# Sums of the out projection's weight blocks: made in SBUF beside the product, or all in DRAM during attention

## The chip, the cores and the metric

The kernel runs on one core of a Trainium2 chip. The metric is the device time of one execution in microseconds (us). PE is the matrix engine, DVE the vector engine, ACT the scalar engine, POOL the GpSimd engine, SP the engine that issues most DMAs; DMA stands for the 16 DMA engines that serve the core.

## The reference, cut to what matters

One layer with sliding-window attention, then a gated embedding and a norm; everything is float32, with 512 tokens and a model width of 2048:

```python
hn = rmsnorm(x, norm_g)
q, k, v, gate = jnp.split(hn @ swa_w_in, ...)
out = attention(q, k, v, window=128, relative bias, sinks)
x = x + (out * jax.nn.silu(gate)) @ swa_w_out        # the out projection
emb = p @ ple_proj
g = jax.nn.sigmoid(rmsnorm(x, ple_norm) @ ple_gate)
x = x + emb * g
return rmsnorm(x, final_g)
```

## The kernel before

**Products.** Each float32 operand is split into a high part (rounded to the type that PE multiplies) and a low part (the rest), and a product is three matmuls: high by high, high by low, low by high. The high part of a weight piece is a cast on ACT (line 668, tile bhi), the low part a subtraction on DVE (line 669, tile blo). A piece is 128 x 1024 floats, 512 KB. The activations' parts are called fho and flo in the out projection (forms, lines 919 and 920).

**Fewer products by sums.** The out projection and the gate product of the embedding (PLE) are made by Strassen's scheme in Winograd's form: seven products of half-sized matrices in place of eight. Weight quarters are written (row, column): product 1 takes quarter (1,1), 2 takes (2,1), 3 takes (2,2), product 7 takes (1,2) + (2,2), 6 takes sum 7 + (1,1), 5 takes (1,1) + (1,2), 4 takes sum 6 + (2,1). The forms of the activations are differences to match. In the out projection the scheme is applied once more inside product 2 and inside product 4: their smaller products are the steps "m" (product 2) and "n" (product 4), seven products of two pieces each.

**Stages.** Until about 60 us the keys, values and first queries are made. From there to about 450 us the query and gate projections run on PE, and from about 100 us the attention of 64 blocks runs between their matmuls. The weight pieces of these projections (tile wraw, 60 of them, three places) are loaded by SP (line 101), cast on ACT (whi, line 107) and subtracted on DVE (wlo, line 113). From 452 to about 617 us stands the out projection, then PLE to the end.

**Sums in DRAM.** While attention runs, `sum_weights(n)` is called, 102 calls spread evenly over the 64 blocks. Even calls issue a copy of a 512 KB piece from DRAM to DRAM on SP (line 627), odd calls a DMA on POOL that adds another piece to that copy (line 629), three pairs later. So are made the sums 7, 5 and 6 of the out projection, sums 7 and 5 of PLE, and the small sums that the steps "m" need: 48 copies and 48 adds.

**Sums in SBUF.** The rest is made during the out projection. Sum 6 is loaded into eight tiles (grown, kind "seed"); four steps after a tile's use a DMA on POOL adds quarter (2,1) to it (`Inside.grow`, line 740), which makes sum 4. Ten more DMAs on POOL (lines 750 and 760) then make the sums for the steps "n" from these tiles, so that those pieces (kind "part") need no load.

**The order.** The list OUT holds the 68 pieces of the out projection in order: large products (tuples) take 12 matmuls a piece, "m" and "n" six. `Pieces.get(i)` returns the split piece i, and through `ahead(i)` issues loads up to a few pieces ahead and splits up to two or three pieces ahead. Raw pieces of kind "one" lie in the three places of wraw (tile braw), those of kind "small" in two tiles beside them, "seed" in grown. Split pieces have three places (bhi, blo); from piece 14 on every fourth piece uses one more, `spare`. On PE and SP the order is that of the program. On DVE, ACT and POOL it is that of the program until the eighth piece (`order.close()`), then a scheduler's.

Of the kernel before, what the change touches and what calls it, by code (L numbers as in the profile page):

```python
# [20 lines left out]
P = 128  # L21
# [34 lines left out]
def trunk_kernel(ctx: ExitStack, tc: tile.TileContext, a: dict):  # L56
# [546 lines left out]
    def small_sum(q, first, more):  # L603
        for i in range(2):
            t = small[q, i] = tc.dram_tile([P, WE], F32, name=f"small_{q}_{i}")
            copies.append((t, first(i)))
            adds.append((t, more(i)))

    small_sum(7, lambda i: small_piece(0, 1, i), lambda i: small_piece(1, 1, i))
    small_sum(5, lambda i: small_piece(0, 0, i), lambda i: small_piece(0, 1, i))  # L610
    for nm, p in SUMS:
        if (nm, p) == ("w_out", 5):
            small_sum(6, lambda i: small[7, i], lambda i: small_piece(0, 0, i))
        if (nm, p) == ("w_out", 6):
            small_sum(4, lambda i: small[6, i], lambda i: small_piece(1, 0, i))
        for jj in range(2):
            for m in range(4):
                t = summed[nm, p, jj, m] = tc.dram_tile([P, WE], F32, name=f"{nm}_{p}_{jj}_{m}")
                first = {7: (1, 2), 5: (1, 1)}.get(p)
                copies.append((t, block(nm, *first, jj, m) if first else summed[nm, 7, jj, m]))  # L620
                adds.append((t, block(nm, *{7: (2, 2), 5: (1, 2), 6: (1, 1)}[p], jj, m)))
    SUM_STEPS = 2 * len(copies) + 6

    def sum_weights(i):

        if i % 2 == 0 and i // 2 < len(copies):
            nc.sync.dma_start(*copies[i // 2])
        elif i % 2 == 1 and 0 <= i // 2 - 3 < len(adds):
            nc.gpsimd.dma_start(*adds[i // 2 - 3], accum_op=ALU.add, max_dma_last_dim=8192)

    class Pieces:
# [3 lines left out]
        def __init__(self):  # L635
            self.specs, self.base, self.made, self.grown, self.due = [], {}, {}, {}, []
            self.aside, self.first4, self.last4 = [], 0, 0
# [4 lines left out]
        def _prepare(self, i):  # L642
            kind, src, key = self.specs[i]
            if kind == "grow":
                t = self.grown[key]
                nc.gpsimd.dma_start(t, src, accum_op=ALU.add)
            else:
                if kind == "seed":
                    t = self.grown[key] = rooms[0].tile([P, WE], F32, tag="grown", name=f"grown{i}", bufs=8)
                elif kind == "small":  # L650
                    n = small_place(key)
                    if key in (0, 2):
                        self.aside.append(rooms[0].tile([P, 2, WE], F32, tag="partial", name=f"small{key}", bufs=2))
                    t = self.aside[n // 2][:, n % 2]
                else:
                    t = wpool.tile([P, WE], F32, tag="wraw", name=f"braw{i}")
                nc.sync.dma_start(t.rearrange("p (k c) -> p k c", k=2) if kind == "proj" else t, src)
            self.base[i] = t

        def _split(self, i):  # L660
            kind, whose, key = self.specs[i]
            raw = whose.raw(*key) if kind == "part" else self.base.pop(i)
# [5 lines left out]
            nc.scalar.copy(hi, raw)  # L668
            nc.vector.tensor_sub(lo, raw, hi.bitcast(F32))  # L669
            self.made[i] = tuple([t[:, :512], t[:, 512:]] for t in (hi, lo))  # L670
            if kind == "part":
                whose.split(*key)
# [11 lines left out]
        def ahead(self, i):  # L684

            last = len(self.specs) - 9
            for n in range(max(i, 0), min(i + 6, last) + 1):
                kind = self.specs[n][0]
                if n in self.base or n < self.done or kind in ("grow", "part"):
# [5 lines left out]
                if kind == "small":  # L695
                    sooner = all(self.specs[v][0] != kind or small_place(self.specs[v][2]) != small_place(self.specs[n][2]) for v in self.base)
                    if not sooner:
                        continue
                if sooner or n <= i + (4 if self.first4 <= i < self.last4 - 2 else 3):
                    self._prepare(n)  # L700
            while self.done <= min(i + (3 if self.first4 <= i < self.last4 - 2 else 2), last):
                self._split(self.done)
                self.done += 1

        def get(self, i):
# [3 lines left out]
            if kind in ("seed", "grow"):  # L709
                n = next((n for n in range(i + 1, len(self.specs)) if self.specs[n][2] == key), None)  # L710
                if n is not None:
                    self.due.append((i + 6, partial_of(self._prepare, n)))
                elif key[0] == inside.nm:
                    self.due.append((i + GROW, partial_of(inside.grow, key)))
# [5 lines left out]
    GROW = 4  # L720
    FIRST_SMALL, LAST_SMALL = 14, 46

    def small_place(key):
        return key % 4 if key < 10 else 2 + key % 2

    FOURTH = 14, 68
# [4 lines left out]
    class Inside:  # L731
# [10 lines left out]
        def begin(self):  # L742

            s7 = rooms[0].tile([P, 2, 2, 512], F32, tag="partial", name="sum7", bufs=2)
            self.s7 = s7.rearrange("p i k c -> p i (k c)")
            self.t = {(kh, jj, i): B.grown[self.nm, jj, 2 * kh + i] for kh in range(2) for jj in range(2) for i in range(2)}

        def sums(self):
            for i in range(2):
                nc.gpsimd.dma_start(self.s7[:, i], self.t[1, 1, i])  # L750
                yield
            for i in range(2):
                self.grow_by(self.s7[:, i], self.t[0, 1, i])
                yield
            for i in range(2):
                self.grow_by(self.t[0, 1, i], self.t[0, 0, i])
                yield

        def grow_by(self, out, more):
            nc.gpsimd.dma_start(out, more, accum_op=ALU.add)  # L760

        def raw(self, q, i):
            if q == 7:
                return self.s7[:, i]
            return self.t[{1: (0, 0), 6: (0, 0), 5: (0, 1), 2: (1, 0), 4: (1, 0), 3: (1, 1)}[q] + (i,)]

        def split(self, q, i):
            if q == 1:
                self.grow_by(self.t[0, 0, i], self.s7[:, i])
            elif q == 2:  # L770
                self.grow_by(self.t[1, 0, i], self.t[0, 0, i])
# [62 lines left out]
    def add_stage(nm, order):  # L834
        at = {}
        if nm == inside.nm:
            parts = [(q, i) for q in ORDER_IN for i in range(2)]
            smalls = [(q, i) for q in ORDER_IN for i in range(2)]
            for step in OUT:
                if step == "m":  # L840
                    q, i = smalls.pop(0)
                    raw = {1: (0, 0), 2: (1, 0), 3: (1, 1)}.get(q)
                    B.add("small", small_piece(*raw, i) if raw else small[q, i], 2 * ORDER_IN.index(q) + i)
                    continue
                if step == "n":
                    B.add("part", inside, parts.pop(0))
                    continue
# [5 lines left out]
                B.add("seed" if p == 6 else "one", src, (nm, jj, m) if p == 6 else None)  # L853
# [113 lines left out]
    for _ in range(2 * 2):  # L967
        while splits(2):
            W.split()
        ksteps(8)  # L970
    for e in range(2):
# [10 lines left out]
    for i in range(blocks + 3):  # L982
# [221 lines left out]
    def turns_of(*v):  # L1204
# [7 lines left out]
    seeds = [n for n, spec in enumerate(B.specs) if spec[0] == "seed" and spec[2][0] == inside.nm]  # L1212
    sooner = {v: n for n, v in enumerate(((1,0,1),(1,0,3)))}
    held, coming = {}, []
    inner_sums, inner_forms = inside.sums(), inside.forms()
    extra = {
        (5, 1, 0): [inside.begin, inner_sums, inner_sums], (5, 1, 1): [inner_forms, inner_sums, inner_sums],
        (5, 1, 2): [inner_forms, inner_sums, inner_sums], (5, 1, 3): [inner_forms], (3, 0, 0): [inner_forms],
# [21 lines left out]
    for at, step in enumerate(OUT):  # L1240
        if at == 8:
# [23 lines left out]
        if step in sooner:  # L1265
            B._prepare(seeds[sooner[step]])
# [305 lines left out]
```

## Time and profile before

| | us |
|---|---|
| runs without a profile | 804.85, 805.84, 804.90 |
| their median | 804.9 |
| the profiled execution | 806.73 |
| its span, from the first to the last instruction | 805.0 |
| PE busy in it | 785.0 |
| DVE, ACT, POOL busy | 612.4, 499.6, 169.8 |

The profile is one execution. PE is busy for 98% of the span, and its matmuls are pipelined, so that time is lost where it sits idle, or where its clock was granted at half. "PE o <- ACT bhi" in the waits means that a matmul which writes o waited for the cast that made bhi. DMA share is the mean busy share of the 16 DMA engines; packets of two queues can overlap, so that it goes a little over 1.

### The profile page before, as it was taken

To read this page: it belongs to the slowest core of one execution; us is meant where nothing else is said; L and a number is where in the kernel's file an instruction comes from. 1 tells how busy PE (TensorE), PEld (TensorE's weight loads), DVE (VectorE), ACT (ScalarE), POOL (GpSimd) and SP (SyncE) were. 2 spreads that over 40 slices of the span, in tenths; PEclk is the share of its full clock that TensorE was granted. 3 is DMA by queue.
4 is the path that set the end of the run, shared out by engine and by line. 5 is a ranking of instruction groups with operands and counts; after the bars stand their busy time and mean duration, and the time that the engine had idled before them with its cause. 6 is when DMAs were issued, how large, how long until landed. Compare 5 with 4: busy or idle time off the path is not lost.

```text
span 805.0 us, 11199 instructions
## 1 busy us (share of the span) xinstructions
PE 785.0 (98%) x3738; PEld 653.1 (81%) x3738; DVE 612.4 (76%) x1043; ACT 499.6 (62%) x1016; POOL 169.8 (21%) x384
## 2 busy tenths in 40 slices
PE   9999999999999999999999999959999999999995
PEld 7888888888888888888888888847788888888885
DVE  4445478888868787687876999848798666899885
ACT  5641367677656666566666658526789755667755
POOL 0003014443243414441234103201100020210000
PEclk9999999999999999999999999989999999999998
DMA  8770598999888978898787479999873996885533
GB/s 332 277 214 6 186 250 226 246 254 244 242 258 218 222 230 216 247 247 243 208 230 171 158 278 332 288 266 351 249 214 101 367 220 218 171 222 189 178 105 105
DMA packets 47338, 180.77 MB, mean 225 GB/s; under 512 B 6880, under 2 KB 7520, under 8 KB 42800
## 3 DMA queue, kind: packets, MB, share of 16 engines
q1 hardware_dynamic: 36992, 134.26, 48.0%
q0 software_dynamic: 10000, 45.41, 29.5%
q8 instruction: 29, 0.48, 0.2%
q10 hardware_dynamic: 288, 0.39, 0.2%
q14 instruction: 29, 0.24, 0.1%
HBM read 168.97 MB, written 54.58 MB: 278 GB/s over the span
## 4 chain that ended last, share of the span: by engine, by line
PE 85%; DMA 7%; DVE 4%; issue 1%; ACT 1%; SPq 0%; DVEq 0%; ACTq 0%
PE qps L124 7%; PE qps L126 7%; PE qps L125 7%; PE gps L124 7%; PE gps L125 7%; PE gps L126 7%; PE g L126 5%; PE g L125 5%; PE g L124 5%; DMA small<-small 4%; PE o L125 3%; DMA grown<-w_out 3%; PE o L126 3%; PE o L124 3%; PE s L401 2%; PE o L523 2%
## 5 line engine op out<-in xcount | busy, mean ns | idle before, releaser
L669 DVE TENSOR_TENSOR blo<-braw,bhi 128x1024 fp32r<-128x1024 f32 x68 | 83.3, 1225 | 32.9 <-ACT bhi L668 32.5
L668 ACT CAST bhi<-braw 128x1024 fp32r<-128x1024 f32 x68 | 71.5, 1053 | 58.9 <-DMA braw<-w_out 16.7
L124 PE MATMUL gps<-xh,whi 128*128 128x512 f32 x256 | 100.5, 393 | 0.0
L125 PE MATMUL gps<-xl,whi 128*128 128x512 f32 x256 | 100.0, 391 | 0.0
L126 PE MATMUL gps<-xh,wlo 128*128 128x512 f32 x256 | 99.9, 390 | 0.0
L503 POOL TENSOR_SCALAR_AFFINE_SELECT own<-r 64x256 fp32r<-64x256 f32 x96 | 60.7, 632 | 184.8 <-ACT r L484 102.5
L113 DVE TENSOR_TENSOR wlo<-wraw,whi 128x1024 fp32r<-128x1024 f32 x60 | 73.5, 1226 | 25.0 <-ACT whi L107 23.6
L124 PE MATMUL qps<-xh,whi 128*128 128x512 f32 x224 | 87.7, 392 | 0.0
L125 PE MATMUL qps<-xl,whi 128*128 128x512 f32 x224 | 87.4, 390 | 0.0
L126 PE MATMUL qps<-xh,wlo 128*128 128x512 f32 x224 | 87.4, 390 | 0.0
L461 ACT ACTIVATE t<-t,sm 128x129 f32<-128x129 f32 x128 | 50.6, 397 | 49.2 <-DVE sm L452 46.4
L124 PE MATMUL g<-bhi,fhg 128*128 128x512 f32 x192 | 75.2, 392 | 0.0
L126 PE MATMUL g<-bhi,flg 128*128 128x512 f32 x192 | 74.8, 390 | 0.0
L125 PE MATMUL g<-blo,fhg 128*128 128x512 f32 x192 | 74.7, 389 | 0.0
L107 ACT CAST whi<-wraw 128x1024 fp32r<-128x1024 f32 x60 | 62.1, 1037 | 15.4 <-DMA wraw<-in_w_q 15.4
L124 PE MATMUL o<-bhi,fho 128*128 128x512 f32 x132 | 52.4, 397 | 7.2 <-ACT bhi L668 7.2
L484 ACT CAST r<-pt 128x256 fp32r<-128x256 f32 x64 | 23.8, 372 | 55.7 <-PE pt L479 55.3
L126 PEld LDWEIGHTS gps<-xh,wlo 128*128 128x128 f32 x256 | 48.1, 188 | 10.6
L124 PEld LDWEIGHTS gps<-xh,whi 128*128 128x128 f32 x256 | 48.1, 188 | 9.0
L125 PEld LDWEIGHTS gps<-xl,whi 128*128 128x128 f32 x256 | 48.1, 188 | 8.7
L125 PE MATMUL o<-blo,fho 128*128 128x512 f32 x132 | 52.7, 400 | 1.6 <-DVE blo L669 1.6
L126 PE MATMUL o<-bhi,flo 128*128 128x512 f32 x132 | 52.0, 394 | 0.0
(276 smaller groups left out, 1893.3 us busy)
## 6 DMA issues: line engine op xcount, KB each, us to landing
wraw<-in_w_gate_in SPq DMA_DIRECT2D x32, 512.0 KB, 5.9
wraw<-in_w_q SPq DMA_DIRECT2D x28, 512.0 KB, 6.1
w_out<-in_w_out POOLq DMA_DIRECT2D x24, 512.0 KB, 7.8
braw<-in_ple_gate SPq DMA_DIRECT2D x24, 512.0 KB, 4.2
w_out<-in_w_out SPq DMA_DIRECT2D x16, 512.0 KB, 8.2
ple_gate<-in_ple_gate SPq DMA_DIRECT2D x16, 512.0 KB, 7.0
ple_gate<-in_ple_gate POOLq DMA_DIRECT2D x16, 512.0 KB, 7.2
braw<-in_w_out SPq DMA_DIRECT2D x16, 512.0 KB, 4.1
```

What stands on the lines that cost most here:

```text
L107: nc.scalar.copy(hi, self.raw[i])
L113: nc.vector.tensor_sub(lo, raw, hi.bitcast(F32))
L124: nc.tensor.matmul(ps, sh, mh, start=first, stop=False, skip_group_check=more)
L125: nc.tensor.matmul(ps, sh, ml, start=False, stop=False, skip_group_check=more)
L126: nc.tensor.matmul(ps, sl, mh, start=False, stop=last, skip_group_check=more)
L401: nc.tensor.matmul(s_ps[:, u, : 2 * n], st, key[:, :, first : first + n], start=True, stop=True)
L461: nc.scalar.activation(su, su, AF.Exp, bias=sm[:, u : u + 1], accum_out=sm[:, 2 + u : 3 + u])
L484: nc.scalar.copy(r[:, 0], PT[i])
L503: nc.gpsimd.affine_select(out=cols(own[places[g % 2 ^ low]]), in_=cols(r[here, low].bitcast(F32)), pattern=[[sign * QB, 2], [0, GROUP], [s ...
L523: nc.tensor.matmul(out, first, r[:, low], start=low == 0, stop=own is None and low == 1)
L668: nc.scalar.copy(hi, raw)
L669: nc.vector.tensor_sub(lo, raw, hi.bitcast(F32))
```

## The change

All sums of the out projection are made in DRAM during attention, those of sum 4 and of the steps "n" too: 62 copies and 64 adds (two of the sums are added in place, into a piece of sum 4 that nothing reads any more). Of the now 134 calls of `sum_weights` eight stand ahead of the attention, and 126 are spread over its 64 blocks. The pieces 4 to 67 are plain loads into a ring of eight places (tile ring, in the space of the grown tiles), up to nine pieces ahead, as places come free. `Inside` keeps only the forms. The extra place `spare` serves from piece 6 on, and the program's order holds on DVE, ACT and POOL to the twentieth piece.

```diff
-    def small_sum(q, first, more):
+    def sum_of(first, more, nm):
+        t = tc.dram_tile([P, WE], F32, name=nm)
+        copies.append((t, first))
+        adds.append((t, more))
+        return t
+    def small_sum(of, q, first, more):
         for i in range(2):
+            small[of, q, i] = sum_of(first(i), more(i), f"small_{of}_{q}_{i}")
+    def large_sum(nm, p, only=range(2)):
+        for jj in only:
             for m in range(4):
+                summed[nm, p, jj, m] = sum_of(
+                    block(nm, *first, jj, m) if first else summed[nm, 7 if p == 6 else 6, jj, m],
+                    block(nm, *{7: (2, 2), 5: (1, 2), 6: (1, 1), 4: (2, 1)}[p], jj, m),
...
+    large_sum("w_out", 5)
+    large_sum("w_out", 4)
+    large_sum("ple_gate", 7, (0,))
+    small_sum(4, 7, lambda i: large_piece(1, 1, i), lambda i: large_piece(0, 1, i))
+    for i in range(2):
+        small[4, 5, i] = large_piece(0, 1, i)
+        copies.append(None)
+        adds.append((small[4, 5, i], large_piece(0, 0, i)))
...
-    SUM_STEPS = 2 * len(copies) + 6
+    SUM_START = 8
+    SUM_REST = 2 * len(copies) + 6 - SUM_START
...
+                elif FIRST_RING <= i < LAST_RING:
+                    t = rooms[0].tile([P, WE], F32, tag="grown", name=f"ring{i}", bufs=8)
...
-            for n in range(max(i, 0), min(i + 6, last) + 1):
+            for n in range(max(i, 0), min(i + REACH, last) + 1):
...
-                if kind == "one" and FIRST_SMALL <= n < LAST_SMALL:
-                    sooner = sum(self.specs[v][0] == "one" for v in self.base) < 3
+                if FIRST_RING <= n < LAST_RING:
+                    sooner = len(rooms) > 0
...
-    FOURTH = 14, 68
+    FIRST_RING, LAST_RING, REACH = 4, 68, 9
+    FOURTH = 6, 68
...
-        def grow(self, key):
-            nm, jj, m = key
-            nc.gpsimd.dma_start(B.grown[key], block(nm, 2, 1, jj, m), accum_op=ALU.add)
...
-        def sums(self):
-            for i in range(2):
-                nc.gpsimd.dma_start(self.s7[:, i], self.t[1, 1, i])
...
-                B.add("seed" if p == 6 else "one", src, (nm, jj, m) if p == 6 else None)
+                B.add("one", src)
...
-            for n in range(i * SUM_STEPS // blocks, (i + 1) * SUM_STEPS // blocks):
-                sum_weights(n)
+            for n in range(i * SUM_REST // blocks, (i + 1) * SUM_REST // blocks):
+                sum_weights(SUM_START + n)
...
-        if at == 8:
+        if at == 20:
             order.close()
```

**SP during attention, around the load of the last block of biases.** A row is a DMA, out<-in, with the program's tile numbers; `w_out_4_1_2` is a piece of sum 4, `small_4_7_0` a small sum for the steps "n". Before:

```order
L101 DMA wraw41_3407<-in_w_gate_in 128x1024
L627 DMA ple_gate_7_0_0_778<-in_ple_gate 16x8192
L101 DMA wraw42_3471<-in_w_gate_in 128x1024
L101 DMA wraw43_3533<-in_w_gate_in 128x1024
L627 DMA ple_gate_7_0_1_779<-in_ple_gate 16x8192
L627 DMA ple_gate_7_0_2_780<-in_ple_gate 16x8192
L101 DMA wraw44_3655<-in_w_gate_in 128x1024
```

and now:

```order
L101 DMA wraw41_3444<-in_w_gate_in 128x1024
L652 DMA ple_gate_7_0_3_789<-in_ple_gate 16x8192
L101 DMA wraw42_3508<-in_w_gate_in 128x1024
L652 DMA small_4_7_0_790<-w_out_4_1_2_784 16x8192
L101 DMA wraw43_3571<-in_w_gate_in 128x1024
L652 DMA small_4_7_1_791<-w_out_4_1_3_785 16x8192
L101 DMA wraw44_3692<-in_w_gate_in 128x1024
```

The copies stand denser between the loads of wraw, and two of those shown here read a sum that POOL's adds finished shortly before.

On POOL the eighteen DMAs of lines 740, 750 and 760 are gone from the out projection; only the four that add the input stay there, ahead of PLE's.

**DVE, at the fourth to seventh piece of the out projection.** `gate` and `fg` are subtractions that make forms, `flo` and `pTl` low parts of forms. Before:

```order
L669 TENSOR_TENSOR blo4_5045<-braw4_5018,bhi4_5044 128x1024
L920 TENSOR_TENSOR flo7_01_5061<-gate0_1697,fho7_01_5060 128x512
L812 SCALAR_TENSOR_TENSOR pTl_4992<-gate2_3998,pTh_4991 128x512
L907 TENSOR_TENSOR gate0_1697<-gate2_3998,gate0_1697 128x4x256
L669 TENSOR_TENSOR blo5_5067<-braw5_5042,bhi5_5066 128x1024
L907 TENSOR_TENSOR gate1_2862<-gate1_2862 128x4x256
L669 TENSOR_TENSOR blo6_5090<-braw6_5064,bhi6_5089 128x1024
```

and now:

```order
L781 TENSOR_TENSOR fg_5034<-gate2_4036,gate3_4629 128x512
L690 TENSOR_TENSOR blo4_5099<-ring4_5045,bhi4_5098 128x1024
L895 TENSOR_TENSOR flo7_01_5115<-gate0_1723,fho7_01_5114 128x512
L690 TENSOR_TENSOR blo5_5121<-ring5_5047,bhi5_5120 128x1024
L882 TENSOR_TENSOR gate1_2896<-gate1_2896 128x4x256
L690 TENSOR_TENSOR blo6_5142<-ring6_5049,bhi6_5141 128x1024
```

One small subtraction moved ahead of piece 4, and two form instructions moved from before piece 5 to later places.

More of the change, by code (lines that the diff above doesn't have):

```diff
@@ L601, in small_piece, with large_piece @@
         return block("w_out", 2, 1, jj, 2 * kh + i)
-    def small_sum(q, first, more):
-        for i in range(2):
[L605 to L616, printed above, removed]
+    def large_piece(kh, jj, i):
+        return summed["w_out", 4, jj, 2 * kh + i]
@@ L619, in trunk_kernel @@
                 first = {7: (1, 2), 5: (1, 1)}.get(p)
-                copies.append((t, block(nm, *first, jj, m) if first else summed[nm, 7, jj, m]))
-                adds.append((t, block(nm, *{7: (2, 2), 5: (1, 2), 6: (1, 1)}[p], jj, m)))
-    SUM_STEPS = 2 * len(copies) + 6
+                summed[nm, p, jj, m] = sum_of(
+                    block(nm, *first, jj, m) if first else summed[nm, 7 if p == 6 else 6, jj, m],
+                    block(nm, *{7: (2, 2), 5: (1, 2), 6: (1, 1), 4: (2, 1)}[p], jj, m),
+                    f"{nm}_{p}_{jj}_{m}",
+                )
@@ new lines, in trunk_kernel @@
+    small_sum(2, 7, lambda i: small_piece(0, 1, i), lambda i: small_piece(1, 1, i))
+    small_sum(2, 5, lambda i: small_piece(0, 0, i), lambda i: small_piece(0, 1, i))
+    large_sum("w_out", 7)
+    small_sum(2, 6, lambda i: small[2, 7, i], lambda i: small_piece(0, 0, i))
+    large_sum("w_out", 6)
+    small_sum(2, 4, lambda i: small[2, 6, i], lambda i: small_piece(1, 0, i))
+    large_sum("w_out", 5)
+    large_sum("w_out", 4)
+    large_sum("ple_gate", 7, (0,))
+    small_sum(4, 7, lambda i: large_piece(1, 1, i), lambda i: large_piece(0, 1, i))
@@ L624, in sum_weights @@
+    for i in range(2):
+        small[4, 5, i] = large_piece(0, 1, i)
+        copies.append(None)
+        adds.append((small[4, 5, i], large_piece(0, 0, i)))
+    large_sum("ple_gate", 7, (1,))
+    small_sum(4, 6, lambda i: small[4, 7, i], lambda i: large_piece(0, 0, i))
+    large_sum("ple_gate", 5, (0,))
+    small_sum(4, 4, lambda i: small[4, 6, i], lambda i: large_piece(1, 0, i))
+    large_sum("ple_gate", 5, (1,))
+    SUM_START = 8
+    SUM_REST = 2 * len(copies) + 6 - SUM_START
     def sum_weights(i):
@@ L626, in sum_weights @@
         if i % 2 == 0 and i // 2 < len(copies):
-            nc.sync.dma_start(*copies[i // 2])
+            if copies[i // 2]:
+                nc.sync.dma_start(*copies[i // 2])
         elif i % 2 == 1 and 0 <= i // 2 - 3 < len(adds):
@@ L636, in __init__ @@
             self.specs, self.base, self.made, self.grown, self.due = [], {}, {}, {}, []
-            self.aside, self.first4, self.last4 = [], 0, 0
+            self.first4, self.last4 = 0, 0
         def add(self, kind, srcs, key=None):
@@ L660, in _split @@
         def _split(self, i):
-            kind, whose, key = self.specs[i]
-            raw = whose.raw(*key) if kind == "part" else self.base.pop(i)
+            raw = self.base.pop(i)
             if self.first4 <= i < self.last4 and i % 4 == 3:
@@ L670, in _split @@
             self.made[i] = tuple([t[:, :512], t[:, 512:]] for t in (hi, lo))
-            if kind == "part":
-                whose.split(*key)
         def split_last(self, k, hi, lo):
@@ L686, in ahead @@
             last = len(self.specs) - 9
-            for n in range(max(i, 0), min(i + 6, last) + 1):
+            for n in range(max(i, 0), min(i + REACH, last) + 1):
                 kind = self.specs[n][0]
-                if n in self.base or n < self.done or kind in ("grow", "part"):
+                if n in self.base or n < self.done or kind == "grow":
                     continue
-                if kind == "one" and FIRST_SMALL <= n < LAST_SMALL:
-                    sooner = sum(self.specs[v][0] == "one" for v in self.base) < 3
+                if FIRST_RING <= n < LAST_RING:
+                    sooner = len(rooms) > 0
                 else:
                     sooner = kind == "seed" and n <= i + 6
[L695 to L699, printed above, removed]
+                if sooner or n <= i + 3:
                     self._prepare(n)
@@ L719, in trunk_kernel @@
     B = Pieces()
[L720 to L724, printed above, removed]
-    FOURTH = 14, 68
+    FIRST_RING, LAST_RING, REACH = 4, 68, 9
+    FOURTH = 6, 68
     FINAL_G = 6
@@ L736, in __init__ @@
             self.nm, self.made = nm, {}
-        def grow(self, key):
-            nm, jj, m = key
-            nc.gpsimd.dma_start(B.grown[key], block(nm, 2, 1, jj, m), accum_op=ALU.add)
[L742 to L746, printed above, removed]
-        def sums(self):
-            for i in range(2):
-                nc.gpsimd.dma_start(self.s7[:, i], self.t[1, 1, i])
[L751 to L771, printed above, removed]
         def forms(self):
@@ L842, in add_stage @@
                     raw = {1: (0, 0), 2: (1, 0), 3: (1, 1)}.get(q)
-                    B.add("small", small_piece(*raw, i) if raw else small[q, i], 2 * ORDER_IN.index(q) + i)
+                    B.add("one", small_piece(*raw, i) if raw else small[2, q, i])
                     continue
                 if step == "n":
-                    B.add("part", inside, parts.pop(0))
+                    q, i = parts.pop(0)
+                    raw = {1: (0, 0), 2: (1, 0), 3: (1, 1)}.get(q)
+                    B.add("one", large_piece(*raw, i) if raw else small[4, q, i])
                     continue
@@ L965, in splits @@
         return len(W.made) <= min(at // 8 + ahead, len(W.srcs) - 1)
-    for _ in range(2 * 2):
+    for n in range(2 * 2):
         while splits(2):
@@ L970, in trunk_kernel @@
         ksteps(8)
+        for v in range(SUM_START // 4):
+            sum_weights(n * (SUM_START // 4) + v)
     for e in range(2):
@@ L1211, in trunk_kernel @@
     smalls = small_forms(small_made)
-    seeds = [n for n, spec in enumerate(B.specs) if spec[0] == "seed" and spec[2][0] == inside.nm]
-    sooner = {v: n for n, v in enumerate(((1,0,1),(1,0,3)))}
     held, coming = {}, []
-    inner_sums, inner_forms = inside.sums(), inside.forms()
+    inner_forms = inside.forms()
     extra = {
-        (5, 1, 0): [inside.begin, inner_sums, inner_sums], (5, 1, 1): [inner_forms, inner_sums, inner_sums],
-        (5, 1, 2): [inner_forms, inner_sums, inner_sums], (5, 1, 3): [inner_forms], (3, 0, 0): [inner_forms],
+        (5, 1, 1): [inner_forms], (5, 1, 2): [inner_forms], (5, 1, 3): [inner_forms], (3, 0, 0): [inner_forms],
         (3, 0, 1): [partial_of(turn, 0, 0, "o")],
@@ L1264, in trunk_kernel @@
             load_x(x_at[step])
-        if step in sooner:
-            B._prepare(seeds[sooner[step]])
         if p in ahead and (p != 5 or seen2 >= 10):
```

8 lines of the change are left out of this document (removed).

## The prediction

> **What bounds the kernel now.** I read the page's first part, then PE by stage, then what PE waited for, and from there backwards.
>
> ```profile
> span 805.0 us, 11199 instructions
> PE 785.0 (98%) x3738; PEld 653.1 (81%) x3738; DVE 612.4 (76%) x1043; ACT 499.6 (62%) x1016; POOL 169.8 (21%) x384
> ```
>
> PE is the bound: whatever is gained must come out of the 20 us in which it is idle, or out of matmuls at a low clock. Busy time by stage (engine us and count, then the granted clock, DMA share and GB/s moved) shows where those are:
>
> ```profile
> core 0: us, PE busy (x) PEld busy (x) DVE busy (x) ACT busy (x) POOL busy (x), PEclk, DMA share, GB/s
> 0.00:60.00 60.00, 58.70 (x295) 49.55 (x296) 27.29 (x41) 33.57 (x44) 3.15 (x10) 1.00 0.82 276
> 60.00:100.00 40.00, 40.00 (x184) 33.28 (x183) 20.25 (x36) 10.93 (x15) 8.52 (x30) 1.00 0.31 97
> 100.00:450.00 350.00, 350.00 (x1737) 293.63 (x1737) 277.81 (x607) 227.78 (x625) 123.60 (x305) 1.00 0.85 231
> 450.00:500.00 50.00, 50.00 (x223) 41.33 (x223) 47.49 (x58) 31.59 (x43) 4.55 (x5) 1.00 0.77 264
> 500.00:530.00 30.00, 30.00 (x134) 24.65 (x133) 24.02 (x28) 16.19 (x20) 8.23 (x9) 1.00 1.07 282
> 530.00:550.00 20.00, 11.15 (x38) 7.72 (x37) 9.21 (x10) 7.59 (x10) 1.10 (x2) 0.74 1.04 319
> 550.00:580.00 30.00, 29.32 (x128) 23.16 (x127) 23.49 (x29) 19.10 (x31) 4.30 (x5) 1.00 0.97 287
> ...
> 620.00:790.00 170.00, 170.00 (x766) 140.99 (x765) 139.02 (x177) 113.17 (x162) 13.79 (x16) 1.00 0.70 202
> 790.00:805.00 15.00, 5.82 (x49) 5.62 (x47) 7.79 (x24) 5.33 (x11) 0.00 (x0) 0.79 0.43 140
> ```
>
> Attention and PLE have no idle PE at all. The start loses 1.3 us and the tail 9.2, which the change leaves alone. Between 530 and 580 us, in the middle of the out projection, PE loses 8.85 + 0.68 = 9.5 us, and its clock drops. What it waited for, of the whole stretch from 100 to 790 us:
>
> ```profile
> PE o L124 <- ACT bhi L668: 7.2, 1, 7.2
> PE o L125 <- DVE blo L669: 2.3, 4, 0.7
> ```
>
> One wait of 7.2 us for a cast, and small ones for the subtraction behind it. In the timeline of PE the matmuls after it start 0.43 us apart:
>
> ```profile
> 541.51 0.80 PE L124 MATMUL o<-bhi,fho 128*128 128x512 f32 x1 [7.21 <-ACT bhi L668]
> ...
> 544.22 0.63 PE L125 MATMUL o<-blo,fho 128*128 128x512 f32 x1
> 544.64 0.63 PE L126 MATMUL o<-bhi,flo 128*128 128x512 f32 x1
> ```
>
> and the clock in two cuts of 5 us there is at half:
>
> ```profile
> 536.00:541.00 5.00, 0.00 (x0) 0.00 (x0) 0.00 (x0) 0.58 (x1) 0.00 (x0) 0.50 1.05 275
> 541.00:546.00 5.00, 4.02 (x9) 2.84 (x10) 2.79 (x3) 2.79 (x4) 0.00 (x0) 0.50 1.03 344
> ```
>
> The cast came late because its raw piece did. ACT in the same stretch sits idle before one cast after the other, each time for a load:
>
> ```profile
> 522.90 1.05 ACT L668 CAST spare<-small 128x1024 fp32r<-128x1024 f32 x1 [1.29 <-DMA small<-in_w_out]
> 526.75 1.05 ACT L668 CAST bhi<-braw 128x1024 fp32r<-128x1024 f32 x1 [2.26 <-DMA braw<-w_out]
> 530.51 1.05 ACT L668 CAST bhi<-small 128x1024 fp32r<-128x1024 f32 x1 [2.71 <-DMA small<-small]
> 540.41 1.04 ACT L668 CAST bhi<-braw 128x1024 fp32r<-128x1024 f32 x1 [8.85 <-DMA braw<-w_out]
> ```
>
> And the loads are late because the DMA engines are full, with POOL's adds into SBUF in the first place. The DMAs issued between 500 and 540 us, by queue (packets, MB, share of the 16 engines) and by issue (median us to landing):
>
> ```profile
> q0 software_dynamic: 1771, 5.17, 66.2%
> q1 hardware_dynamic: 1769, 5.96, 40.2%
> grown<-in_w_out POOLq DMA_DIRECT2D x7, 512.0 KB, 22.2
> braw<-w_out SPq DMA_DIRECT2D x4, 512.0 KB, 24.5
> ```
>
> q0 carries POOL's DMAs, q1 the loads. The two move the same number of packets, but q0's take 66% of the engines. The loads get 5.96 MB in 40 us, 149 GB/s. There the pieces alternate between twelve matmuls and six; 18 matmuls at 134 in 30 us are 4.03 us, and two pieces of 0.524 MB in that time are 260 GB/s. So a load takes 24.5 us, and PE runs out of pieces.
>
> **The change, part by part.** *The stall.* The eight adds into grown and the ten DMAs for the steps "n" leave this stage. By queue, from 450 to 600 us, with one issue:
>
> ```profile
> q1 hardware_dynamic: 8576, 29.89, 53.7%
> q0 software_dynamic: 3503, 10.94, 36.2%
> braw<-in_w_out SPq DMA_DIRECT2D x12, 512.0 KB, 3.9
> ```
>
> A POOL DMA of 0.524 MB costs 150 x 0.362 / 10.94 x 0.524 = 2.6 us of all engines, a load 150 x 0.537 / 29.89 x 0.524 = 1.4. Eighteen of the first go (47 us) and about fourteen loads more come (20 us): 135 us of busy time become 108, in a stage that is then 137 us long, a share of 0.79 where now 1.07 stands for 30 us and more. With eight places each load also has seven pieces' time, 9 to 19 us, to land; the twelve plain loads from in_w_out in these 150 us landed in 3.9. (How many come into the stage more is an estimate from the order of SP.) So I let the stall go whole. In matmuls: at 4.47 per us, 20 us should hold 89.3 and hold 38, and 30 us should hold 134 and hold 128. That is 57.3 matmuls, **12.8 us**; 9.5 of it is idle time, the other 3.3 the half clock. What is late next is DVE.
>
> *DVE's order.* From 450 to 500 us DVE is busy 47.49 of 50 us. The change adds nothing to its work. One subtraction comes ahead of piece 4, form work moves away from piece 5, and the extra place from piece 6 lets splits run further ahead. The nearest rows:
>
> ```profile
> 463.18 0.68 DVE L812 SCALAR_TENSOR_TENSOR pTl<-gate,pTh 128x512 fp32r<-128x512 f32 x1
> 463.78 1.22 DVE L907 TENSOR_TENSOR gate<-gate,gate 128x1024 f32<-128x1024 f32 x1
> ```
>
> One instruction of 0.68 us comes sooner, 1.9 us move back. Bounds: a further gain of 0.5 us (what small waits my count may miss), or a loss if DVE, in written order, waits where the scheduler filled in: four instructions like the second, 4.9 us. I take a loss of 0.4, since both moves are small beside the 2.7 us that PE spends on a piece, and since before piece 20 there was no wait to lose.
>
> *The sums in attention.* This is the price. 14 more copies on SP, 16 more adds on POOL; of these 11 and 15 fall into the 350 us of attention, the rest ahead of it, where the DMA share is 0.31. The queues from 100 to 450 us:
>
> ```profile
> q1 hardware_dynamic: 11152, 55.35, 46.4%
> q0 software_dynamic: 3840, 25.17, 38.3%
> ```
>
> the 50 us of it with the highest share:
>
> ```profile
> 150.00:200.00 50.00, 50.00 (x253) 42.02 (x252) 40.91 (x90) 35.16 (x98) 21.56 (x54) 1.00 0.94 247
> ```
>
> and the loads of wraw, with what they waited for and how long they took:
>
> ```profile
> L107 ACT CAST whi<-wraw x53: 1029/1034/1051, 105.2 to 439.7; 128x1024 fp32r<-128x1024 f32 x53
>   ACT whi L107: 9.9, 15
> DMA to landing us min/median/max: 3.4/6.0/11.6
> ```
>
> An add costs 350 x 0.383 / 48 = 2.8 us of all engines, a copy 350 x 0.464 / 55.35 x 0.524 = 1.54. So 15 x 2.8 + 11 x 1.54 = 59 us are added, and the share goes from 0.85 to 1.02; 1.07 was held in the out projection. In bytes, 231 GB/s become 231 + 26 x 0.524 / 350 = 270, and the row at 1.07 moved 282. It is full, but it fits. What would feel it first are the loads of wraw. A cast comes every 334.5 / 52 = 6.4 us; a load goes out when the piece three before it is split, so 3 x 6.4 less some 2.3 us for cast and subtraction, 17 us, ahead of its use. It lands in 6.0, at worst 11.6: a margin of 11 and 5.4 us. No cast waited for a load (the only wait in the wraw rows is DVE's for ACT). I put this at **nothing**, with the margin as the cover; if that is used up, every further us of lateness is a us of PE, which is the second rival. Below nothing it cannot go, since PE has no idle time there.
>
> SP is in order, so that copies which wait for a sum hold the wraw loads queued behind them. The closest pair is `small_4_7_0`, 5 calls or 2.5 blocks behind its add: 2.5 x 5.5 (350 us for 64 blocks) = 13.7 us against the landing of an add:
>
> ```profile
> ple_gate<-in_ple_gate POOLq DMA_DIRECT2D x16, 512.0 KB, 7.2
> w_out<-in_w_out POOLq DMA_DIRECT2D x24, 512.0 KB, 7.8
> ```
>
> About 6 us to spare there, and a wait would take from a margin of 5 to 11. POOL's own adds stand 3.5 blocks behind their copies instead of 4.4, 19 us against a landing of about 8: behind a waiting add stand the selects of the next block, which PE needs, but there is room.
>
> **Sum.** The profiled execution took 806.7 us: 806.7 - 12.8 + 0.4 = 794.3. It lies 1.8 over the median of the runs, 804.9, so the forecast for the median is 792.5.
>
> **The rivals.** *DVE takes over* (partly faster). For it: 47.49 of 50 us busy at the stage's start. Against it: no PE wait there. Price: four instructions of 1.22 us, 4.9 us at most: 797.
>
> *Attention's transfers do not fit* (slower). Mechanism: adds and copies queue up faster than the 16 engines take them, wraw lands ever later, and PE waits for each piece. For it: the stage's share comes to 1.02, and 0.94 is the most that 50 us of it show, at 247 GB/s. If that is its limit, 270 / 247 x 350 = 383 us of transfers, 33 late, less the median margin of 11: 22 us of PE waits, 792.5 + 22 = 814. Against it: 1.07 in the out projection. It makes the kernel slower from a lateness of 12.4 + 11 = 23 us on, a limit of 270 x 350 / 373 = 253 GB/s.
>
> *The memory, not the engines, is the limit* (slower). Copies and adds touch DRAM at least twice per byte: now 80.5 MB + 25.17 + 47 x 0.524 = 130 MB in 350 us, 372 GB/s, then 27 MB more. If 372 were all, 157 MB would take 422 us, 72 late, less 11: 854. Against it: nothing says that 372 is a ceiling; at 150 to 200 us the engines moved more than the mean, and PE did not wait. The Trainium skill, "DMA: Bandwidth & Descriptors", section Specifications, gives about 358 GB/s of HBM for one core. By that rule the stage would take 157 / 0.358 = 439 us. The trace does not agree: it has carried 372 for 350 us with PE busy throughout.
>
> *It does not do what it says* (no change): the loads are late for another reason, say SP's order, and the stall comes again: 804.9. Against it: equal packets in both queues while q0 holds 66% of the engines.
>
> **How the numbers follow.** Stall gone and all else hidden: 0.64, at 791 to 794.5. DVE takes over, or attention leaks a few us of waits: 0.12, at 795 to 803. No change: 0.04. Transfers do not fit: 0.17, since no stretch of the attention shows a share of 1.02. Memory: 0.03. The time is that of the first. The range must hold 8 in 10: the first two hold 0.76, no change the rest, so 791 to 805.5. About 0.2%, 1.6 us, is what a measurement of this kernel tells from no change. Faster 0.76, same 0.04, slower 0.20.
>
> **What would show it.** Right: no PE wait between 450 and 600 us; q0 almost empty there, loads landing in 4 to 8 us; a DMA share near 1 from 100 to 450 us with PE still busy 350 of 350; wraw landing in 7 to 11 us, no cast waiting for it. Wrong: waits "whi <- DMA wraw" that grow through the attention, followed by PE waits and a clock below 1.00 before 450 us; waits of PE for blo from 455 to 500 us with DVE busy throughout, for the first rival; SP waiting long before `small_4_7_0`, POOL before an add.

## The result and the profile after

The changed kernel takes 792.1 us (median of 6 runs, 791.8 to 792.53), the kernel before 804.96: a ratio of 0.983, 95% interval 0.982 to 0.985. The forecast was 792.5. The first lines of the page of the changed kernel:

```profile
span 790.2 us, 11240 instructions
PE 780.0 (99%) x3738; PEld 652.3 (83%) x3738; DVE 612.9 (78%) x1043; ACT 499.6 (63%) x1016; POOL 175.8 (22%) x382
```

The span is 14.8 us shorter, and PE is idle for 10.2 us in all, at the start and in the tail. The same cuts as before show what happened in between (engine us and count, granted clock, DMA share, GB/s):

```profile
0.00:60.00 60.00, 58.78 (x299) 49.65 (x299) 28.42 (x42) 34.65 (x46) 5.70 (x13) 1.00 0.84 276
60.00:100.00 40.00, 40.00 (x184) 33.32 (x183) 19.60 (x35) 10.66 (x18) 14.01 (x32) 1.00 0.61 185
100.00:450.00 350.00, 350.00 (x1738) 293.81 (x1737) 277.85 (x608) 226.94 (x621) 137.31 (x318) 1.00 0.96 266
...
150.00:200.00 50.00, 50.00 (x254) 42.05 (x253) 40.26 (x90) 34.73 (x97) 22.91 (x52) 1.00 1.02 284
...
450.00:500.00 50.00, 50.00 (x224) 41.36 (x223) 45.11 (x52) 29.77 (x39) 1.48 (x2) 1.00 0.80 270
500.00:530.00 30.00, 30.00 (x134) 24.87 (x133) 28.99 (x35) 21.38 (x28) 3.65 (x3) 1.00 1.03 326
530.00:550.00 20.00, 20.00 (x90) 16.56 (x89) 19.14 (x23) 13.55 (x21) 0.00 (x0) 1.00 0.83 284
550.00:580.00 30.00, 30.00 (x139) 24.86 (x138) 25.23 (x31) 22.93 (x38) 0.00 (x0) 1.00 0.74 250
```

From 530 to 580 us PE is busy throughout at full clock, with 90 + 139 matmuls where 38 + 128 stood. The DMAs issued from 500 to 540 us say why. By queue and by issue, as before:

```profile
q1 hardware_dynamic: 3425, 11.53, 77.6%
q0 software_dynamic: 816, 1.57, 22.6%
ring<-w_out SPq DMA_DIRECT2D x10, 512.0 KB, 7.7
ring<-in_w_out SPq DMA_DIRECT2D x6, 512.0 KB, 4.7
ring<-small SPq DMA_DIRECT2D x4, 512.0 KB, 8.9
```

POOL's queue q0 fell from 5.17 MB and 66.2% to 1.57 MB and 22.6% (what is left is the input x). The loads got 11.53 MB in these 40 us instead of 5.96, and they landed in 4.7 to 8.9 us, by the medians of the ring's three groups, where the loads of weights took 16.7 to 24.9 before. The price stands in attention. The wraw loads there, from 100 to 450 us (idle time before the instructions, then time to landing), and the one cast that waited for a load:

```profile
  ACT whi L107: 11.4, 15
  DMA wraw<-in_w_q: 1.5, 1
...
DMA to landing us min/median/max: 4.6/7.6/18.4
```

```profile
194.07 1.05 ACT L107 CAST whi<-wraw 128x1024 fp32r<-128x1024 f32 x1 [1.46 <-DMA wraw<-in_w_q]
```

PE did not wait, but the slowest landing went from 11.6 to 18.4 us. The load that this cast waited for was issued at 176.5 us and took 17.6 us to land.

### The profile page after: what moved, and what is told of

Same layout as the page of the kernel before. It is cut to its first block, busy times and chain, and to the rows that moved or that the text cites. A ratio compares the mean times of both kernels' runs of the same rounds, so it can differ in the third digit from the quotient of the medians.

```text
span 790.2 us, 11240 instructions
## 1 busy us (share of the span) xinstructions
PE 780.0 (99%) x3738; PEld 652.3 (83%) x3738; DVE 612.9 (78%) x1043; ACT 499.6 (63%) x1016; POOL 175.8 (22%) x382
## 2 busy tenths in 40 slices
DMA packets 48490, 194.41 MB, mean 246 GB/s; under 512 B 7296, under 2 KB 7936, under 8 KB 42704
## 3 DMA queue, kind: packets, MB, share of 16 engines
HBM read 187.85 MB, written 70.31 MB: 327 GB/s over the span
## 4 chain that ended last, share of the span: by engine, by line
PE 98%; DMA 0%; DVE 0%; ACT 0%; issue 0%; DVEq 0%
PE gps L124 7%; PE gps L125 7%; PE gps L126 7%; PE qps L124 7%; PE qps L125 7%; PE qps L126 7%; PE o L126 6%; PE o L124 6%; PE o L125 6%; PE g L126 6%; PE g L125 6%; PE g L124 6%; PE s L401 2%; PE o L523 2%; PE vps L228 2%; PE pt L479 2%
## 5 line engine op out<-in xcount | busy, mean ns | idle before, releaser
L503 POOL TENSOR_SCALAR_AFFINE_SELECT own<-r 64x256 fp32r<-64x256 f32 x96 | 62.4, 650 | 162.3 <-ACT r L484 80.2
L689 ACT CAST bhi<-braw 128x1024 fp32r<-128x1024 f32 x44 | 46.4, 1057 | 36.1 <-PE g L126 20.5
L690 DVE TENSOR_TENSOR blo<-braw,bhi 128x1024 fp32r<-128x1024 f32 x44 | 54.1, 1229 | 18.5 <-ACT bhi L689 18.3
L690 DVE TENSOR_TENSOR blo<-ring,bhi 128x1024 fp32r<-128x1024 f32 x48 | 58.3, 1223 | 6.6 <-ACT bhi L689 6.2
L689 ACT CAST bhi<-ring 128x1024 fp32r<-128x1024 f32 x48 | 50.2, 1050 | 20.4 <-PE o L126 16.8
L671 POOL DMA_DIRECT2D grown<-in_ple_gate x16 | 13.7, 854 | 176.4 <-DMA grown<-ple_gate 119.8
```

What stands on the lines that cost most here:

```text
L503: nc.gpsimd.affine_select(out=cols(own[places[g % 2 ^ low]]), in_=cols(r[here, low].bitcast(F32)), pattern=[[sign * QB, 2], [0, GROUP], [s ...
```

## The experiments

**What made the stall: POOL's adds, the read-ahead, or the order?** Four kernels take these apart. Their edits are cut to the lines that matter. The first keeps everything of before but the order:

```diff
-        if at == 8:
+        if at == 20:
             order.close()
```

> The kernel before, with the written order of the out projection kept to piece 20 instead of piece 8, nothing else. Theory (the stall comes from POOL's adds into SBUF that fill the DMA engines while the pieces are loaded): no change, 804 to 807 us, one PE wait of about 7 us near 541 us as before. Rival (the order of DVE and ACT in the stage carries part of the gain): 794 to 802 us.

Measured: 806.34 us, ratio 1.0019 (1.0009 to 1.0029). No gain, as the theory said; the median is 1.4 us later. The stall is there in another shape: PE waits for casts twice, 4.4 us together, where one wait of 7.2 was, and runs longer at the low clock. From 530 to 580 us it has 50 + 120 matmuls, against 38 + 128. The stage in the kernel with the later close:

```profile
450.00:500.00 50.00, 48.79 (x216) 39.82 (x215) 43.06 (x49) 27.54 (x36) 3.25 (x4) 1.00 0.81 274
500.00:530.00 30.00, 30.00 (x134) 24.84 (x133) 29.33 (x35) 20.99 (x28) 8.90 (x9) 1.00 1.07 279
530.00:550.00 20.00, 14.33 (x50) 10.26 (x49) 7.75 (x8) 6.92 (x10) 1.10 (x2) 0.87 1.05 301
```

The order also makes a new wait of 1.2 us at 450 to 500 us.

The second leaves POOL's DMAs out and keeps the rest:

```diff
         def grow(self, key):
-            nc.gpsimd.dma_start(B.grown[key], block(nm, 2, 1, jj, m), accum_op=ALU.add)
+            pass
         def grow_by(self, out, more):
-            nc.gpsimd.dma_start(out, more, accum_op=ALU.add)
+            pass
```

(the two copies into sum 7 go as well, and the pieces that stood in sum 7 are read from a grown tile)

> The kernel before, without the 18 DMAs that POOL issues in the out projection for the steps n (eight adds into grown, two copies into sum7, eight adds after it), so that those pieces are read unsummed; this part of the result is left out. Loads, their read-ahead, casts, subtractions and matmuls are as before. Theory (adds fill the engines): the stall goes, 791 to 794 us, loads at 500 to 540 us land in 4 to 8 us instead of 22 to 29. Rival (the read-ahead of three or four pieces is too short, whatever POOL does): the stall stays for the most part, 801 to 806 us.

Measured: 792.87 us, ratio 0.985 (0.983 to 0.987). The whole stall goes with the eighteen DMAs. Loads, read-ahead, casts, subtractions and matmuls are those of before; besides the engines' time, the waits of these DMAs for grown tiles are gone too, but what the stalled cast had waited for was a plain load. The windows, and two lines for the DMAs issued from 500 to 540 us:

```profile
500.00:530.00 30.00, 30.00 (x134) 24.83 (x134) 27.37 (x32) 19.25 (x24) 2.42 (x2) 1.00 0.96 313
530.00:550.00 20.00, 20.00 (x90) 16.58 (x89) 18.23 (x22) 13.92 (x21) 0.00 (x0) 1.00 0.66 211
```

```profile
q0 software_dynamic: 768, 1.47, 19.9%
braw<-w_out SPq DMA_DIRECT2D x7, 512.0 KB, 4.1
```

Loads of braw from w_out, which took 24.5 us before, land in 4.1; those of small pieces, at 9.2 and 10.3 us, are a little over the 4 to 8 expected.

The third keeps the sums in DRAM, but not the ring:

```diff
-    FIRST_RING, LAST_RING, REACH = 4, 68, 9
+    FIRST_RING, LAST_RING, REACH = 0, 0, 9
-                if sooner or n <= i + 3:
+                if sooner or n <= i + (4 if self.first4 <= i < self.last4 - 2 else 3):
```

> The changed kernel without the ring of eight places: pieces go through the three places of wraw, three pieces ahead (four in the stretch with the extra place), as before; all sums stay in DRAM. Theory (adds fill the engines): no adds there, so 792 to 794 us, PE waits under 1 us from 450 to 600 us. Rival (the read-ahead is what mattered): waits of PE come back, 797 to 806 us.

Measured: 810.64 us, ratio 1.009 (1.006 to 1.012): slower than before, and beyond the rival's range. With none of the eighteen DMAs about, the engines are not full and the loads are fast, and still ACT waits for them. Windows, the landing of braw's loads in 500 to 560 us, and the longest of ACT's waits from 450 to 620 us:

```profile
450.00:500.00 50.00, 50.00 (x224) 41.33 (x223) 43.70 (x50) 27.87 (x36) 1.54 (x2) 1.00 0.67 212
500.00:530.00 30.00, 25.66 (x99) 18.93 (x98) 20.28 (x24) 17.11 (x23) 3.65 (x3) 0.94 0.84 235
530.00:550.00 20.00, 18.32 (x77) 13.68 (x76) 17.95 (x22) 10.58 (x14) 0.00 (x0) 1.00 0.81 274
```

```profile
DMA to landing us min/median/max: 3.3/4.4/8.9
```

```profile
ACT bhi L689 <- DMA braw<-w_out: 20.7, 15, 3.5
ACT spare L689 <- DMA braw<-w_out: 8.0, 7, 2.0
ACT bhi L689 <- DMA braw<-in_w_out: 7.0, 7, 2.0
```

A place is held for a load (4.4 us), a cast (1.05) and a subtraction (1.22), together 6.7 us, so three places give a piece each 2.2 us. PE takes two pieces in 4.03 us, 2.0 each, from piece 20 to 46. In the kernel before, seeds and small pieces had places of their own, eight and four, and the steps "n" needed no load at all; that this spared it the same wait is an inference, which no run tests. The fourth kernel tests the count: four places in use (each piece takes two of the eight).

```diff
-    FIRST_RING, LAST_RING, REACH = 4, 68, 9
+    FIRST_RING, LAST_RING, REACH = 4, 68, 5
+                    rooms[0].tile([P, WE], F32, tag="grown", name=f"skip{i}", bufs=8)
                     t = rooms[0].tile([P, WE], F32, tag="grown", name=f"ring{i}", bufs=8)
```

> The changed kernel with a ring of four places in use instead of eight (read-ahead of five pieces instead of nine). In the run without a ring a place was held for a load (4.3 us) and cast and subtraction (2.3 us), some 6.8 us with the gaps, so that three places gave a piece each 2.3 to 2.4 us where PE takes 2.0 at pieces 20 to 46. Theory (places by holding time): four places give one each 1.7 us, enough on the mean, so 792 to 796 us with PE waits of 0 to 3 us. Rival (the depth of eight is needed because single loads come late): 797 to 806 us.

Measured: 791.99 us (791.89 to 792.1), no wait of PE in the stage. Four places at 1.7 us a piece do what eight do, so the theory of places by holding time holds.

**What is the written order to piece 20 worth?** Back to piece 8, first without and then with the extra place from piece 6 (the edit of the first is shown; the second keeps the line of FOURTH):

```diff
-    FOURTH = 6, 68
+    FOURTH = 14, 68
-        if at == 20:
+        if at == 8:
             order.close()
```

> The changed kernel with written order only to piece 8 and the extra place from piece 14, as before. Theory: 791.5 to 793 us, no PE wait in the stage; the lead of the splits over PE at pieces 4 to 13, up to 5.7 us now, falls back to 0.2 to 3 us. Rival (DVE's order is worth something either way): 790 or 796 us.

> The changed kernel with written order only to piece 8, the extra place from piece 6 as in the change. With both undone PE waited 1.1 us for the subtraction of piece 4. Theory (the order of DVE makes that wait): 793.0 to 793.5 us, the wait is there again. Rival (the extra place does): 791.8 to 792.4 us, no wait.

Measured: 793.2 and 793.46 us. My theory for the first (no wait, at most 793) falls, if narrowly, and neither time of its rival came; that for the second (the order makes the wait) holds. Both show the same PE wait, here from 450 to 600 us of the first:

```profile
PE o L125 <- DVE blo L690: 1.1, 1, 1.1
```

It stands at piece 4, whose subtraction the written order brings forward. So the written order saves 1.1 us of waits in this kernel, and made 1.2 in the one before: it fits a program, it is not better by itself.

**How near is attention to its limit?** Copies and adds of 512 KB into DRAM places that nobody reads, called at the end of each block. An add goes to the place of the copy before, so that 8 copies bring 7 adds and 16 bring 15, one add fewer than the expectations say:

```diff
+    def extra_sums(i):
+        if i * MORE // 64 < (i + 1) * MORE // 64:
+            t = tc.dram_tile([P, WE], F32, name=f"more{i}")
+            nc.sync.dma_start(t, block("w_out", 1, 1, i % 2, i // 2 % 4))
+            more.append(t)
+            if len(more) > 1:
+                nc.gpsimd.dma_start(more[-2], block("w_out", 2, 2, i % 2, i // 2 % 4), accum_op=ALU.add, max_dma_last_dim=8192)
```

> The changed kernel with 8 copies and 8 adds of 512 KB more, into DRAM places that nobody reads, spread evenly over the 64 blocks of attention. At 1.44 us a copy and 2.74 us an add (of all 16 engines) they take 33 us of 350, 0.95 of share on top of 9.6 tenths: 0.96 becomes 1.06. Theory (the engines carry up to about 1.07, and loads of wraw have 5 to 11 us of cover before PE): 792 to 794 us, some casts wait for wraw, no PE wait above 1 us. Rival (attention was at its limit already, its loads at 176 to 209 us had no slack left): PE waits at 180 to 220 us, 796 to 810 us.

> As the run with 8 more, but 16 copies and 16 adds: 67 us of the engines, a share of 1.15 where 1.07 is the most that a stage has shown. Theory (1.07 is the limit): (1.15 - 1.07) x 350 = 28 us late at the end, less some 12 us of slack and lead: 16 us of PE waits before 450 us, about 808 us (800 to 820). Rival (the limit is higher, or the queues only grow): 792 to 796 us.

Measured: 799.14 us (798.15 to 803.13) with 8 and 825.76 (823.18 to 830.06) with 16. The theory of a limit at 1.07 falls twice: the rival held at 8, and 16 cost twice what I gave, 33.7 us. The stage from 100 to 450 us with 8, then with 16:

```profile
100.00:450.00 350.00, 346.30 (x1704) 289.80 (x1703) 271.12 (x597) 222.63 (x614) 139.75 (x322) 0.99 1.00 284
```

```profile
100.00:450.00 350.00, 333.65 (x1591) 275.45 (x1590) 253.99 (x562) 206.87 (x573) 141.08 (x304) 0.97 1.01 288
```

The share stops at 1.00 and 1.01, at 284 and 288 GB/s. With 16, PE is idle for 16.35 us, about the 16 that I gave as waits; but the stage holds 147 matmuls fewer than the changed kernel's 1738, which is 29.6 us at that kernel's rate. The clock, 0.97 on the mean of 350 us, makes up some 10 us of the rest by my estimate: a wait of PE costs more than its length. How a late load reaches PE is to be read in the timelines of ACT and PE of the run with 8:

```profile
192.33 0.18 ACT L461 ACTIVATION_READ_ACCUMULATOR t<-t,sm 128x1 f32 x1
200.16 1.04 ACT L107 CAST whi<-wraw 128x1024 fp32r<-128x1024 f32 x1 [7.64 <-DMA wraw<-in_w_q]
201.11 0.36 ACT L484 CAST r<-pt 128x256 fp32r<-128x256 f32 x1
...
202.27 0.70 ACT L471 ACTIVATE t<-t,sm 128x128 f32<-128x128 f32 x2
```

```profile
202.73 0.77 PE L479 MATMUL pt<-ident,t 128*128 128x128 f32 x2 [2.99 <-ACT t L471]
```

PE does not wait for the weight, but for the softmax work (L471) that stands behind the waiting cast in ACT's queue. The cast is late by 7.64 us, PE idle for 3.7 (2.99 here and 0.7 in a next wait), and the clock is at 0.53 from 205 to 210 us. Over the stage 34 matmuls are missing, 6.8 us, which is nearly the whole cost of 7.0. Three more kernels place the same 15 DMAs elsewhere (the edit, against the run with 8, is below), or make up about the same engine time otherwise:

```diff
-        if i * MORE // 64 < (i + 1) * MORE // 64:
+        if i >= 24 and (i - 24) * MORE // 40 < (i - 23) * MORE // 40:
```

> The changed kernel with the same 8 copies and 8 adds more as in the run that took 799, but all in blocks 24 to 63, from about 230 us on, none in the stretch at 155 to 210 us where its wait arose (one cast waited 7.6 us for a load issued at 176 us). Theory (the fullest 50 us set the price, not the sum over attention): 791.8 to 794 us. Rival (the mean share of the 350 us decides): 797 to 802 us.

> The changed kernel with 23 copies of 512 KB more (no add), spread evenly over attention: 23 x 1.44 = 33 us of the engines, as much as 8 copies and 8 adds. Theory (engine time is what is short, whoever takes it): 797 to 802 us, as there. Rival (the adds hurt more than their engine time, since they come in a queue of their own and the wraw loads share with it): 792 to 795 us.

> The changed kernel with 2 copies and 11 adds of 512 KB more, spread evenly (the copies in blocks 0 and 1): 2 x 1.44 + 11 x 2.74 = 33 us of the engines. Theory (engine time is what is short): 797 to 802 us. Rival (adds hurt more than their engine time): 803 us or more; a second rival (copies hurt more, since they stand in SP's order ahead of the wraw loads): 792 to 796 us.

Measured: 797.89 (794.26 to 799.72), 803.19 (801.44 to 803.96) and 798.35 us (797.91 to 800.23). Late in attention they cost about as much (5.8 us), so the theory of the fullest 50 us falls and its rival held: the wait at 200 us is not one weak place, it goes elsewhere with the DMAs.

```profile
400.00:450.00 50.00, 46.80 (x225) 38.24 (x225) 36.03 (x75) 30.58 (x82) 21.36 (x48) 1.00 1.01 284
```

The stage from 100 to 450 us with 23 copies, then with 11 adds:

```profile
100.00:450.00 350.00, 344.88 (x1684) 287.66 (x1683) 269.33 (x595) 219.13 (x606) 131.65 (x312) 0.99 1.00 292
```

```profile
100.00:450.00 350.00, 345.45 (x1698) 288.24 (x1698) 269.96 (x596) 221.74 (x610) 143.56 (x325) 1.00 1.01 280
```

Adds (6.3 us) and the mixture (7.0) cost about the same for about the same engine time. Copies alone cost 11.1 us, 4 to 5 more than either, which neither the theory nor its rivals had. It is not that a copy takes more than the 1.44 us that I took from the mean of its queue: the copies are the packets of 32 KB, and in this run 1272 of them took 29.0% of the engines' time from 100 to 450 us, 1.28 us a copy. By the packets' own times (an add is 2.7 us) the 23 copies are 29 us of the engines, the 8 copies and 7 adds 29 and the 2 copies and 11 adds 32. So engine time alone does not set the price. That copies hold the wraw loads behind them in SP's queue would fit, and no run shows it: the landings of wraw have a median of 12.8 us here against 11.1 and 11.2, but the casts' waits for them (15.1 us) are hardly longer than with the adds (14.3).

Last, the part of the change that lies ahead of attention is undone:

```diff
-    SUM_START = 8
+    SUM_START = 0
```

> The changed kernel with no sum step ahead of attention: all 134 steps over the 64 blocks, so 4 copies and 4 adds more in attention, 4 x 1.44 + 4 x 2.74 = 17 us of the engines, half of what cost 7 us in the run with 8 and 8. Theory (attention is within a few pairs of its limit): 793 to 797 us, casts wait 2 to 6 us for wraw between 170 and 210 us, PE waits or stays just covered. Rival (some 4 us of cover in ACT's queue take it all): 791.8 to 792.6 us.

Measured: 795.12 us (794.06 to 796.13), as the theory said.

```profile
100.00:450.00 350.00, 348.62 (x1724) 291.44 (x1723) 275.10 (x604) 225.83 (x620) 136.04 (x320) 1.00 0.99 274
```

In this stretch stand 61 copies and 63 adds, against 57 and 60 in the changed kernel: four copies and three adds cost 3.0 us. The first eight steps, which I had not given a price, keep the change at its full gain.

No version beat the changed kernel; four places do the same with half the ring.

## Why the prediction was right, and where its steps were off

*The stall goes whole*: shown, and its cause too, by the run without the adds. The share of the stage was forecast at 0.79, and from 450 to 600 us the two queues now take 71.7% and 8.0%. The term was a little small: 229 matmuls in 50 us is 4.58 per us, and 63 more of them are 13.8 us, not the 12.8 that came from the rate ahead of the stall. Another 0.9 us of the span's 14.8 lies in the first 60 us (299 matmuls for 295); the kernel of before with the later close had 299 there as well, so this is a matter of the one profiled run of before, which lay 1.8 over its median. For the profiled executions the sum was 2.4 us too high (794.3 forecast, 791.93 measured): about 1.0 in the stall, 0.9 at the start and the 0.4 of DVE's order. Taking off 1.8 for the median then brought 792.5 close to the 792.1 measured, although the changed kernel's profiled run lies at its median. The mechanism was right; that the time fits to 0.4 us is in part luck.

*Eight places give each load 9 to 19 us*: told beside the adds as if it were a comfort. It is a condition, that there be more than three. Sums in DRAM turn fourteen pieces into loads and take away the places of their own that seeds and small pieces had; without the ring that loses 18.5 us, more than the adds had cost. I had no rival for it. But it is not the eight that matter: four would do.

*DVE's order costs 0.4*: wrong in sign. From 450 to 530 us PE is busy 80 of 80 us, and in this kernel the older order costs 1.1 to 1.4 us (793.2 and 793.46 against 792.1).

*The sums in attention cost nothing*: right in the time, wrong in the reason. Forecast were a share of 1.02 and 270 GB/s, measured 0.96 and 266: the sum was good to 6%. Half of that is a count: 10 copies and 12 adds more came into the stretch, not 11 and 15, since four adds were issued before 100 us, and with these my prices give 0.99. But I took landings of 7 to 11 us and no cast waiting; the median went to 7.6, the slowest to 18.4, and one cast waited 1.5 us. The lead of 17 us was about right, as the load of 17.6 us shows; the landing was mis-sized. A median landing says little where the queues are full. And "every further us is a us of PE" left out some 4 us before PE runs out of work (7.64 late, 3.7 idle), which fits that the wait of 1.5 did not reach PE. Once it does reach it, the clock takes most of that back: those 7.64 us cost 7.0. The 1.07 that I held against the rival was carried in a stage whose loads took 24.5 us to land: it was no proof of capacity.

*Attention's transfers do not fit* (0.17): the mechanism is real and was missed narrowly. With 7, 15 and 31 DMAs more it costs 3, 7 and 34 us. Its limit is not the 247 GB/s that I gave it, but 280 to 292, by the mix of adds and copies.

*The memory is the limit* (0.03): the run carried more than the 372 GB/s that this rival took for a ceiling: with 93.07 MB moved, 32.12 of them in adds, and 57 copies of 0.524 counted twice, 155 MB in 350 us, 443 GB/s. The page's own count over the whole span bears this way of counting out: it has 187.85 MB read from HBM and 70.31 written, 258.2, and the 194.41 MB moved with 126 copies and adds of 0.524 once more are 260.5. The Trainium skill, "DMA: Bandwidth & Descriptors", Specifications, gives the 358 as half of a stack's 716 GB/s, shared out between two cores; this run of one core went above it, so it was no ceiling here.

## What to carry to other kernels

Full DMA queues are relieved by moving their work to where the engines have room, but count what the move takes away: places and pieces that needed no load. A ring needs at least as many places as the time that one is held (landing, cast, subtraction) divided by the time of a piece, rounded up: here 6.7 by 2.0, four. And a stage in which PE is never idle can still be a few transfers from its edge: read the slowest landing and the first cast that waits, not the median.

## What was not expected of the hardware

That the same share means so different a thing: in attention PE began to wait between 266 GB/s (0.96) and 274 GB/s (0.99, the run with no step ahead), while in the out projection 326 to 328 GB/s went through at 1.00 to 1.03 without a wait of PE. There most of it was plain loads (11.53 of 13.13 MB from 500 to 540 us); from 100 to 450 us adds alone held 48.0% of the engines' time. An add of 512 KB took 2.7 us of the engines and a copy 1.3. So the share alone doesn't tell how late the next load will be.
